# A two-batch encoder layer on one core: the prompt's down-projection joined with the sample's seven products, the sample's convolution as three half-rate filters, the gate's tanh in PSUM

## The chip, the core and the metric

The kernel runs on one core of a Trainium2 chip. A core has a matrix engine (TensorE, PE in the profile), which writes to PSUM, and engines for elementwise work: VectorE (DVE), ScalarE (ACT) and GpSimd (POOL). SyncE (SP) issues most DMA transfers. Each engine takes its own instructions in order and waits on semaphores for the others. The metric is the time of one execution on the device in microseconds; less is better.

## The reference, cut to what matters

One layer of an encoder runs for two batches with the same weights: a prompt of 512 tokens and a sample of 1024. The model width is 1024, the FFN width 2816. Everything is float32.

```python
def _trunk(x, ...):
    h = _rmsnorm(x, norm_attn_g)
    z = h @ w_in                                   # q, k, v, ca, cb
    a_out = _window_attn(q, k, v, bias, band, attn_sink)     # |q-k| <= 128, 8 heads, 2 kv heads
    c = ca * sigmoid(cb)
    c = _dwconv(c, conv_dw_w, conv_dw_b)           # depthwise, 31 taps, 512 channels
    c = silu(_layernorm(c, conv_ln_g, conv_ln_b))
    x = x + concatenate([a_out, c], -1) @ w_out
    h = _rmsnorm(x, norm_ffn_g)
    u = _dwconv(h @ w_up, ffn_dw_w, ffn_dw_b)      # depthwise, 3 taps, 2 * 2816 channels
    x = x + (silu(u[..., :2816]) * u[..., 2816:]) @ w_down
    return _rmsnorm(x, norm_final_g)
y = _trunk(x_prompt, ...), _trunk(x_sample, ...)
```

## The kernel before

**Precision.** Each matrix product is done as three matmuls in a reduced float32 format (F32R): both operands are split into a rounded part `hi` (a copy on ACT) and a rest `lo` (a subtraction on POOL or DVE), and hi x hi, hi x lo and lo x hi are added up in PSUM. A matmul takes 128 rows of the contracted dimension and 512 columns.

**Stages.** The program is one long stream, in this order:

1. Input projections of both batches, weight chunk by weight chunk (`proj`, L288 to L290), with the prompt's convolution and attention mixed in, then the prompt's output projection (`out_half`, L733 to L735).
2. The prompt's FFN: 22 slices of 128 channels (`ffn_step`). A slice has two up-projections of 24 matmuls each (`up_half`), a 3-tap convolution on ACT and DVE (L906, L902), and the gate (`gate`, L920 to L925): tanh on ACT, two steps on DVE or POOL, then the split. Every second slice, `down` multiplies the last two slices with their rows of w_down for 4 blocks of 128 tokens and 2 halves of the width (L940 to L942) and adds each result onto `x1` on DVE (L943). `ffn_end` does the last two slices and normalises and stores the prompt's output.
3. The sample's output projection (blocks of 128 tokens), the norms of its convolution (`conv_norm`, L694 to L717) and the splits of w_out (`split_wo`, L766, L767).
4. The sample's up-projection by a Strassen-Winograd scheme: 7 products of half-size blocks in place of 8 (`first` to `seventh`, all through `prod`, L1167 to L1169). The gate's results and their sums go to DRAM (`ga`).
5. The sample's down-projection by the same scheme: seven products, in the order 1, 2, 5, 6, 7, 4, 3, each over 11 pairs of slices and 4 row blocks (`mm_down`, L1477 to L1479). The operands are loaded back from `ga` and `w_down`, summed and split (`operands`, `split_of`, L1051 to L1055). A product gathers in two wide PSUM tiles of two banks; `evacuate` empties them. There are four wide tiles. The last product is mixed with `finish` (final norm and store).

**Mixing.** In stages 1 and 2 the order is set by counters: `tick()` is called after every two chunks of a projection and after each half block of `down`. Each tick adds `pace["rate"]` to a due count; every full unit advances the generator at the head of `side` by one step (the sample's attention in stage 2, then the loads and splits of w_out, then the first norms). Each tick also adds `pace["late"]` (CD) of credit to the sample's convolution, a generator of single taps.

```python
    pace.update(rate=RD, late=CD)
    for k in range(NJ):
        at[0] = k
        if k == 0:
            side.append(sample())
        ffn_step(k)
    use.update(out=OB, down="b", turn="b")
    pace.update(rate=RE)
    ffn_end(GR[0])
    drain(side)
```

The instructions of an engine are then put in order by a planner that follows this stream by priority with its own estimate of the times; in stage 4 TensorE's order, and in stage 5 TensorE's and SP's, are those of the program. SBUF tiles come from fixed slots (`Slots`), the one that has been free longest first; an instruction that gets a slot waits for its last reader.

**The sample's convolution** (`conv_items`) treats 512 tokens of 128 channels at a time: 24 of the 31 taps on DVE, accumulated in one PSUM bank (L325, L329), 7 as a product on ACT (L317, L320) and an addition on POOL (L321), and a join (L337). Eight such pieces go to DRAM (`cvd`) and are read back block by block by `conv_norm`.

Of the kernel before, what the change touches and what calls it, by code (L numbers as in the profile page):

```python
# [39 lines left out]
RA, RB, RBO, RD, RN, RE = 1.2, 0.8, 2.5, 0.44, 0.8, 0.9  # L40
# [5 lines left out]
NOFF = (4, 7)  # L46

SCB, SCD = "aapa", "vaap"
# [6 lines left out]
FT, PT = 4, (1, 3, 5)  # L55
GP = 1
# [43 lines left out]
def tile_hybrid_encoder(ctx: ExitStack, tc: tile.TileContext, xs, rel_bias, norm_attn_g, w_in,  # L100
# [198 lines left out]
    cvd = {1: dr.tile([P, 4, GR[1]["T"]], F32, name="cvd1")}  # L299
# [4 lines left out]
    def conv_items(g, c, cp):  # L304
        T = GR[g]["T"]
        w = lambda t: cvw[:, t * 4 + c:t * 4 + c + 1]
        cost = 0.13 + NT / 960.0
        noff = NOFF[g]
        off = list(range(CK - noff, CK))
        for n in range(T // NT):  # L310
            src = lambda t: cp[:, t + n * NT:t + (n + 1) * NT]
            pacc = sb.tile([NT])

            def offload(k):
                t = off[k]
                if k == 0:
                    nc.scalar.activation(pacc[:], src(t), AF.Identity, scale=w(t))  # L317
                else:
                    pr = sb.tile([NT])
                    nc.scalar.activation(pr[:], src(t), AF.Identity, scale=w(t))  # L320
                    nc.gpsimd.tensor_tensor(pacc[:], pacc[:], pr[:], op=ALU.add)  # L321

            mid.append((convs, late)[g])
            acc = bank("conv")
            nc.vector.tensor_scalar(acc[:], src(0), w(0), cvb[:, c:c + 1], op0=ALU.mult, op1=ALU.add)  # L325
            yield cost
            k = 0
            for t in range(1, CK - noff):
                nc.vector.scalar_tensor_tensor(acc[:], src(t), w(t), acc[:], op0=ALU.mult, op1=ALU.add)  # L329
                if t % 2 == 1 and k < noff:  # L330
                    offload(k)
                    k += 1
                yield cost
            while k < noff:
                offload(k)
                k += 1
            nc.vector.tensor_tensor(pacc[:], acc[:], pacc[:], op=ALU.add)  # L337
            del acc
            if g == 0:
                kept[c] = pacc  # L340
            else:
                nc.sync.dma_start(cvd[g][:, c, n * NT:(n + 1) * NT], pacc[:])
            mid.clear()
            yield cost

    tanh_t, cpads, kt, vt = {}, {}, {}, {}

    def evac(kind, c, nt, src):
# [9 lines left out]
        elif kind == "ca":  # L358
            if n == 0:
                cp = sb.tile([T + 64])  # L360
                nc.gpsimd.memset(cp[:, 0:PAD], 0.0)
                nc.gpsimd.memset(cp[:, PAD + T:2 * PAD + T], 0.0)
                cpads[g, c] = cp
            cp = cpads[g, c]
            nc.vector.tensor_tensor(src, src, rb[:], op=ALU.mult)
            nc.vector.scalar_tensor_tensor(cp[:, PAD + n * NT:PAD + (n + 1) * NT], tanh_t.pop((nt, c))[:], 1.0, src,
                                           op0=ALU.add, op1=ALU.mult)
# [89 lines left out]
    def landed(i, nt, pp):  # L457
        kind, c, col = order[i]
        evac(kind, c, nt, pp[:])
        if kind == "ca" and nt != 1:  # L460
            g = min(nt, 1)
            (convs, late)[g].append(conv_items(g, c, cpads.pop((g, c))))
        tick()
# [21 lines left out]
    nc.vector.tensor_scalar_mul(cvw[:, :CK * 4], cvw[:, :CK * 4], 0.5)  # L485
    load_rows(1)
# [191 lines left out]
    def conv_norm(i):  # L678
# [6 lines left out]
        else:  # L685
            held = sb.tile([4, P])
            nc.sync.dma_start(held[:], cvd[1][:, :, b * P:(b + 1) * P])
# [23 lines left out]
        for c in range(4):  # L711
            nc.scalar.activation(y[:, c, :], p2[:, c * P:(c + 1) * P], AF.Identity,
                                 scale=lng[:, c:c + 1], bias=lnb[:, c:c + 1])
# [7 lines left out]
    x1d = [dr.tile([P, D], F32, name=f"x1d{i}") for i in range(8)]  # L721

    def out_half(i, n):
# [15 lines left out]
        if n == 1:  # L739
            x1[i] = x  # L740
            if G["g"] == 1:
                nc.sync.dma_start(x1d[i - 4][:], x[:])
# [39 lines left out]
    def make_h2(g, n):  # L782
        ts = []
        for i in range(n * 4, n * 4 + 4):
            k = i if g == 0 else 4 + i
            a = sb.tile([D])
            nc.vector.tensor_scalar_mul(a[:], x1[k][:], rs2[:, k:k + 1])
            ts.append(a)
# [4 lines left out]
    use.update(step="b", turn="a", attn="au", norm="au", out="u")  # L793
# [78 lines left out]
    def want_dn_raw(k):  # L872
        j = seq[k][1]
        dnr[k] = []
        for n in range(2):
            raw = sb.tile([NT])
            nc.sync.dma_start(raw[:], w_down[0, j * P:(j + 1) * P, n * NT:(n + 1) * NT])
            dnr[k].append(raw)

    def want_dn(k):  # L880
        if k in dnr:
            dnw[k] = [split(r) for r in dnr.pop(k)]

# [32 lines left out]
    def gate(ug, uv, pool):  # L916
        gs = []
        for a, b in zip(ug, uv):
            t = sb.tile([NT])
            nc.scalar.activation(t[:], a[:], AF.Tanh, scale=0.5)  # L920
            nc.vector.scalar_tensor_tensor(t[:], t[:], 1.0, a[:], op0=ALU.add, op1=ALU.mult)
            (nc.gpsimd if pool else nc.vector).tensor_tensor(t[:], t[:], b[:], op=ALU.mult)
            hi, lo = sb.tile([NT], F32R), sb.tile([NT], F32R)
            nc.scalar.copy(hi[:], t[:])
            nc.gpsimd.tensor_tensor(lo[:], t[:], hi[:].bitcast(F32), op=ALU.subtract)  # L925
            gs.append((hi, lo))
        return gs

    def down(G, parts, fin):
        base = 4 * G["g"]  # L930
        for tt in range(G["nb"]):
            acc = x1[base + tt]
            c = slice((tt % 4) * P, (tt % 4 + 1) * P)
            for n in range(2):
                pd = bank("down")
                s = slice(n * NT, (n + 1) * NT)
                for x, (gs, wd) in enumerate(parts):
                    hi, lo = gs[tt // 4]
                    wh, wl = wd[n]
                    nc.tensor.matmul(pd[:], hi[:, c], wh[:], start=(x == 0), stop=False)  # L940
                    nc.tensor.matmul(pd[:], hi[:, c], wl[:], start=False, stop=False)
                    nc.tensor.matmul(pd[:], lo[:, c], wh[:], start=False, stop=(x == len(parts) - 1))  # L942
                nc.vector.tensor_tensor(acc[:, s], pd[:], acc[:, s], op=ALU.add)  # L943
                tick()
            if fin is not None:
                ss, rs = sm(2), sm(2)
                o = sb.tile([D])
                for n in range(2):
                    s = slice(n * NT, (n + 1) * NT)
                    nc.scalar.activation(o[:, s], acc[:, s], AF.Square, accum_out=ss[:, n:n + 1])  # L950
                nc.gpsimd.tensor_scalar(rs[:, 0:1], ss[:, 0:1], 1.0 / D, EPS, op0=ALU.mult, op1=ALU.add)
                nc.gpsimd.tensor_scalar(rs[:, 1:2], ss[:, 1:2], 1.0 / D, rs[:, 0:1], op0=ALU.mult, op1=ALU.add)
# [19 lines left out]
    def ffn_step(k):  # L972
# [10 lines left out]
        if j == NJ - 1:  # L983
            want_dn(k)
# [757 lines left out]
```

## Time and profile before

| | |
|---|---|
| median of 3 runs | 1520.96 us (1519.68 to 1521.98) |
| the profiled execution | 1521.1 us, its span 1519.3 us |
| mean granted TensorE clock | 0.997 |
| TensorE busy | 1490.0 us, 98% |
| VectorE, ScalarE, GpSimd busy | 1173.9, 801.8, 737.2 us |
| DMA | 209.71 MB, mean 138 GB/s |

The span runs from the first to the last instruction. Rows of the profile read: line, engine, operation, tile written <- tiles read (names without numbers), shape, count; then the time in which at least one of the group was busy, the mean of one in ns, the engine's idle time before them and who ended it. Tile names are those of the slots: `h` is SBUF of 2048 bytes a partition, `q` of 4096, `c` and `d` others; `a`, `b`, `u`, `c` and `w` are PSUM. Rows of windows give, after the length, the busy time and the count of TensorE, its weight loads, VectorE, ScalarE and GpSimd, then the granted clock, the DMA share and the GB/s. A matmul's own duration overlaps that of the next one.

### The profile page before, as it was taken

Reading aid. Unit: us, or ns where it says so; the run is one execution under the profiler, and the core shown is the slowest. Engines: PE = TensorE matmul, PEld = TensorE weight load, DVE = VectorE, ACT = ScalarE, POOL = GpSimd, SP = SyncE. Lnnn points to the kernel's source line nnn. Section 1 sums busy time; section 2 is a strip of 40 time slices with the busy share of each in tenths; the row PEclk is TensorE's granted clock in tenths of the full one; section 3 lists DMA queues with packets and bytes.
Section 4 is the critical chain, followed back from the end, with each engine's and each line's share of the span. In section 5 each row is a group of like instructions: output and inputs, shape, how many; then the busy total and the mean of one; then the engine's idle time right before and its main releaser. Section 6 shows DMA issues by size and latency. Waiting matters only on the chain. (4 is left out here: it accounts for less than half of the span.)

```text
span 1519.3 us, 20003 instructions
## 1 busy us (share of the span) xinstructions
PE 1490.0 (98%) x6802; PEld 1224.6 (81%) x6802; DVE 1173.9 (77%) x1668; ACT 801.8 (53%) x1419; POOL 737.2 (49%) x649
## 2 busy tenths in 40 slices
PE   8999999899999999999999999999999999999998
PEld 7888778687888778788888888888888888888886
DVE  7877844549999999896575878888888877778794
ACT  6424455447566556655355365544444455454364
POOL 3454353137686777777552325555555554000235
PEclk9999999999999999999999999999999999999999
DMA  9465231823333423335473213333333223396642
GB/s 371 164 166 151 87 101 36 266 97 123 98 112 111 125 91 110 104 113 195 133 258 136 84 56 104 104 105 104 104 105 104 101 94 111 117 393 219 214 146 111
DMA packets 106146, 209.71 MB, mean 138 GB/s; under 512 B 11155, under 2 KB 30739, under 8 KB 105916
## 3 DMA queue, kind: packets, MB, share of 16 engines
q1 hardware_dynamic: 104508, 206.83, 40.9%
q10 hardware_dynamic: 1536, 1.61, 0.3%
q8 instruction: 53, 0.87, 0.2%
q14 instruction: 49, 0.40, 0.1%
HBM read 161.98 MB, written 47.46 MB: 138 GB/s over the span
## 5 line engine op out<-in xcount | busy, mean ns | idle before, releaser
L154 POOL TENSOR_TENSOR q<-q,q 128x1024 fp32r<-128x1024 f32 x66 | 160.2, 2429 | 71.2 <-ACT q L153 34.8
L1051 POOL TENSOR_TENSOR q<-q,q 128x512 fp32r<-128x512 f32 x82 | 114.5, 1408 | 155.7 <-ACT q L1153 151.8
L288 PE MATMUL u<-h,q 128*128 128x512 f32 x384 | 151.7, 395 | 0.1
L290 PE MATMUL u<-h,q 128*128 128x512 f32 x384 | 150.2, 392 | 0.0
L289 PE MATMUL u<-h,q 128*128 128x512 f32 x384 | 150.1, 391 | 0.0
L1167 PE MATMUL w<-h,q 128*128 128x512 f32 x372 | 146.0, 393 | 0.4 <-ACT w L1239 0.4
L1169 PE MATMUL w<-h,q 128*128 128x512 f32 x372 | 144.9, 390 | 0.7 <-POOL q L1051 0.7
L329 DVE SCALAR_TENSOR_TENSOR c<-c,cvw,c 128x512 f32<-128x512 f32 x184 | 137.6, 748 | 1.7
L1168 PE MATMUL w<-h,q 128*128 128x512 f32 x350 | 136.3, 389 | 0.0
L1048 POOL TENSOR_TENSOR q<-q,q 128x1024 f32<-128x1024 f32 x8 | 23.2, 2916 | 177.1 <-DVE q L1048 166.1
L1479 PE MATMUL w<-h,h 128*128 128x512 f32 x264 | 102.7, 389 | 0.0
L1477 PE MATMUL w<-h,h 128*128 128x512 f32 x264 | 102.7, 389 | 0.0
L153 ACT CAST q<-q 128x1024 fp32r<-128x1024 f32 x66 | 69.1, 1050 | 54.6 <-POOL q L154 25.1
L1051 DVE TENSOR_TENSOR h<-h,h 128x512 fp32r<-128x512 f32 (+1 forms) x128 | 89.7, 744 | 9.1 <-ACT h L1055 4.3
L1051 POOL TENSOR_TENSOR c<-q,c 128x512 fp32r<-128x512 f32 x46 | 72.1, 1581 | 49.5 <-ACT c L1153 49.5
L1478 PE MATMUL w<-h,h 128*128 128x512 f32 x244 | 95.1, 390 | 0.6 <-DVE h L1051 0.6
L321 POOL TENSOR_TENSOR h<-h,h 128x512 f32<-128x512 f32 x58 | 76.0, 1311 | 19.5 <-ACT h L320 13.9
L1055 ACT CAST h<-h 128x512 fp32r<-128x512 f32 x101 | 58.9, 618 | 48.6 <-DVE h L1051 27.0
L288 PEld LDWEIGHTS u<-h,q 128*128 128x128 f32 x384 | 72.1, 188 | 15.1 <-DVE h L902 0.6
L1167 PEld LDWEIGHTS w<-h,q 128*128 128x128 f32 x372 | 69.8, 188 | 17.7 <-ACT w L1239 3.7
L290 PEld LDWEIGHTS u<-h,q 128*128 128x128 f32 x384 | 72.1, 188 | 14.7
L289 PEld LDWEIGHTS u<-h,q 128*128 128x128 f32 x384 | 72.2, 188 | 14.0
(459 smaller groups left out, 4355.7 us busy)
## 6 DMA issues: line engine op xcount, KB each, us to landing
q<-in_laid_w_up SPq DMA_DIRECT2D x88, 512.0 KB, 3.6
h<-in_w_down SPq DMA_DIRECT2D x90, 256.0 KB, 3.6
ga<-q SPq DMA_DIRECT2D x65, 256.0 KB, 2.0
h<-ga SPq DMA_DIRECT2D x57, 256.0 KB, 4.3
q<-in_laid_w_in SPq DMA_DIRECT2D x22, 512.0 KB, 4.0
q<-in_x_sample SPq DMA_DIRECT2D x15, 512.0 KB, 6.4
h<-in_laid_w_out SPq DMA_DIRECT2D x28, 256.0 KB, 5.1
h<-qsd SPq DMA_DIRECT2D x24, 256.0 KB, 3.7
```

The lines of the kernel that those rows point to most:

```text
L154: (nc.vector if dve else nc.gpsimd).tensor_tensor(lo[:], raw[:], hi[:].bitcast(F32), op=ALU.subtract)
L288: nc.tensor.matmul(out, whi[:, kc, :], hi[:], start=(kc == 0), stop=False)
L289: nc.tensor.matmul(out, whi[:, kc, :], lo[:], start=False, stop=False)
L290: nc.tensor.matmul(out, wlo[:, kc, :], hi[:], start=False, stop=(kc == KC - 1))
L329: nc.vector.scalar_tensor_tensor(acc[:], src(t), w(t), acc[:], op0=ALU.mult, op1=ALU.add)
L1051: (eng or nc.vector).tensor_tensor(out, a, b, op=ALU.subtract)
L1167: nc.tensor.matmul(out, whi[:, s], hi[:], start=(start and c == 0), stop=False, **go)
L1168: nc.tensor.matmul(out, whi[:, s], lo[:], start=False, stop=False, **go)
L1169: nc.tensor.matmul(out, wlo[:, s], hi[:], start=False, stop=(stop and c == 3), **go)
L1477: nc.tensor.matmul(out, sh[:, c], th[:], start=(p == 0 and not seeded), stop=False, **go)
L1478: nc.tensor.matmul(out, sh[:, c], tl[:], start=False, stop=False, **go)
L1479: nc.tensor.matmul(out, sl[:, c], th[:], start=False, stop=(p == NPAIR - 1), **go)
```

## The change

1. `down` and `ffn_end` are gone. The prompt's gate results go to DRAM (`gap`), in two halves of 256 tokens. While the sample's up-projection runs, `sums_of` forms the sums that the scheme needs from them, on POOL. Each of the seven down products then takes two row blocks of the prompt along (row blocks 4 and 5 in `mm_down`), with a third wide PSUM tile that is opened some steps into the product (`HOLD`; 5 for the first). The prompt's final norm and store move into the last product.
2. The sample's convolution stores its input as even and odd tokens. One filter with the sums of neighbouring taps (16) runs on the odd tokens, two filters (16 and 15 taps) on the differences; each gives 512 outputs and 5 of its taps are offloaded. `conv_norm` puts even and odd outputs back in order.
3. The gate's tanh is written to a PSUM bank, and the step after it works there.
4. Constants: RD 0.44 to 0.55, CAP 48 to 24, and the sample's attention scales one more head on ACT instead of DVE.

```diff
-RA, RB, RBO, RD, RN, RE = 1.2, 0.8, 2.5, 0.44, 0.8, 0.9
+RA, RB, RBO, RD, RN, RE = 1.2, 0.8, 2.5, 0.55, 0.8, 0.9
-SCB, SCD = "aapa", "vaap"
+NOFF = 4
+LOFF = (5, 5, 5)
+SCB, SCD = "aapa", "aaap"
...
+    def late_items(c, cp):
+        odd = lambda m, n=NT: cp[:, 0, m + 1:m + 1 + n]
+        even = lambda m, n=NT: cp[:, 1, m:m + n]
+        ns, no = CK // 2 + 1, CK // 2
+        col = lambda t: cvw[:, t * 4 + c:t * 4 + c + 1]
+        diff = []
+        for k, n in ((0, ns), (1, no)):
+            d = sb.tile([NT + n - 1], among="dq")
+            nc.gpsimd.tensor_tensor(d[:], even(k, NT + n - 1), odd(0, NT + n - 1), op=ALU.subtract)
+            diff.append(d)
+        d = None
+        both = yield from taps(late, odd, lambda s: csum[:, s * 4 + c:s * 4 + c + 1], ns, LOFF[0], with_bias(c))
+        yield 0.13 + NT / 960.0
+        for k, n in ((0, ns), (1, no)):
+            onto = lambda out, x, w: nc.vector.scalar_tensor_tensor(out, x, w, both[:], op0=ALU.mult, op1=ALU.add)
+            y = yield from taps(late, lambda s: diff[k][:, s:s + NT], lambda s: col(2 * s + k), n, LOFF[1 + k], onto)
+            nc.sync.dma_start(cvd[:, c, k, :], y[:])
...
-    def gate(ug, uv, pool):
-        gs = []
-        for a, b in zip(ug, uv):
-            t = sb.tile([NT])
-            nc.scalar.activation(t[:], a[:], AF.Tanh, scale=0.5)
-            nc.vector.scalar_tensor_tensor(t[:], t[:], 1.0, a[:], op0=ALU.add, op1=ALU.mult)
-            (nc.gpsimd if pool else nc.vector).tensor_tensor(t[:], t[:], b[:], op=ALU.mult)
-            hi, lo = sb.tile([NT], F32R), sb.tile([NT], F32R)
...
-    def down(G, parts, fin):
...
-                for x, (gs, wd) in enumerate(parts):
-                    hi, lo = gs[tt // 4]
-                    wh, wl = wd[n]
-                    nc.tensor.matmul(pd[:], hi[:, c], wh[:], start=(x == 0), stop=False)
...
+    def gate(k, a, b):
+        t, pt = sb.tile([2, HT]), bank("gate")
+        nc.scalar.activation(pt[:], a[:], AF.Tanh, scale=0.5)
+        nc.vector.scalar_tensor_tensor(pt[:], pt[:], 1.0, a[:], op0=ALU.add, op1=ALU.mult)
+        nc.vector.tensor_tensor(t[:].rearrange("p h t -> p (h t)"), pt[:], b[:], op=ALU.mult)
+        del pt
+        nc.sync.dma_start(gap[((1, 8), (2, 4))[k % 2]][:, k // 2], t[:])
+
+    def sums_of(p):
+        e, t, x, y = (sb.tile([2, HT]) for _ in range(4))
+        nc.sync.dma_start(e[:], gap[1, 8][:, p])
+        nc.sync.dma_start(t[:], gap[2, 4][:, p])
+        eng = nc.gpsimd
+        eng.tensor_tensor(x[:, 1, :], e[:, 1, :], t[:, 1, :], op=ALU.add)
...
+        nc.sync.dma_start(gap[7, 5][:, p], x[:])
+        nc.sync.dma_start(gap[6, 3][:, p], y[:])
...
-    use.update(out=OB, down="b", turn="b")
+    h2.clear()
+    use.update(out=OB, turn="b")
     pace.update(rate=RE)
-    ffn_end(GR[0])
     drain(side)
...
+        if p % 2 == 0:
+            n = min(2, NPAIR - p) * HT
+            raw = pr.pop((("p", i, 0), p))
+            hi, lo = sb.tile([NT], F32R), sb.tile([NT], F32R)
+            nc.scalar.copy(hi[:, :n], raw[:, :n])
+            sub(lo[:, :n], raw[:, :n], hi[:, :n].bitcast(F32), nc.gpsimd)
+            hp[i, p] = hp[i, p + 1] = hi, lo
...
-    CAP = 48
+    CAP = 24
+    HOLD = 2
     def mm_down(out, i, p, tt, seeded=False):
-        (sh, sl), (th, tl) = hl[i, p]
+        a, (th, tl) = hl[i, p]
         c = slice(tt * P, (tt + 1) * P)
+        if tt > 3:
+            a = hp[i, p]
+            c = slice(p % 2 * HT + (tt - 4) * P, p % 2 * HT + (tt - 3) * P)
...
+        hold = 5 if i == ORDER[0] else HOLD
+        if p == hold:
+            pd.append(wide())
         for tt in range(4):
             mm_down(pd[tt // 2][:, (tt % 2) * NT:(tt % 2 + 1) * NT], i, p, tt)
...
+        if p >= hold:
+            for q in range(p + 1) if p == hold else (p,):
+                for tt in (4, 5):
+                    mm_down(pd[2][:, (tt % 2) * NT:(tt % 2 + 1) * NT], i, q, tt)
+                hl.pop((i, q)), hp.pop((i, q))
```

263 lines of the change are left out of this document (119 added, 144 removed).

## The prediction, on record before the changed kernel ran

> **What bounds the kernel now.** I read, in this order: the page's totals, TensorE's rows one by one, the stages as windows, who waited for whom on TensorE, the groups inside the stage that the diff cuts, and then the seam behind it.
>
> ```profile
> span 1519.3 us, 20003 instructions
> PE 1490.0 (98%) x6802; PEld 1224.6 (81%) x6802; DVE 1173.9 (77%) x1668; ACT 801.8 (53%) x1419; POOL 737.2 (49%) x649
> ...
> 1099.82 0.39 PE L1167 MATMUL w<-h,q 128*128 128x512 f32 x1
> ...
> 1105.94 0.39 PE L1167 MATMUL w<-h,q 128*128 128x512 f32 x1
> ...
> L940 PE MATMUL b<-h,h 128*128 128x512 f32 x144 | 56.5, 396 | 1.7 <-ACT h L153 1.5
> L940 PE MATMUL b<-h,d 128*128 128x512 f32 x32 | 12.8, 405 | 0.2 <-DVE q L943 0.2
> ...
> L1479 PE MATMUL w<-h,h 128*128 128x512 f32 x264 | 102.7, 389 | 0.0
> ```
>
> TensorE is busy 98% of the span, so matmuls are the currency. A matmul lasts 0.39 us but they overlap: from 1099.82 to 1105.94 lie 27 starts, 6.12 / 27 = 0.2267 us each. That, not 0.39, is what one matmul of 512 columns costs the span. L940 stands for the prompt's down-projection: 144 + 32 = 176 rows, and L941 and L942 have as many, 528 matmuls.
>
> ```profile
> 350.00:756.00 406.00, 402.74 (x1868) 332.82 (x1868) 358.31 (x589) 241.69 (x427) 295.37 (x232) 1.00 0.37 120
> 480.00:520.00 40.00, 39.82 (x191) 32.94 (x190) 39.82 (x65) 27.14 (x49) 33.78 (x28) 1.00 0.36 112
> 720.00:756.00 36.00, 36.00 (x163) 29.67 (x161) 16.78 (x23) 12.91 (x20) 19.25 (x12) 1.00 0.37 121
> 1296.00:1513.00 217.00, 216.01 (x951) 177.96 (x949) 167.32 (x228) 104.79 (x193) 40.57 (x37) 1.00 0.57 200
> ...
> PE a L646 <- DVE h L634: 1.6, 2, 1.0
> PE b L940 <- ACT h L153: 1.5, 2, 1.2
> ...
> PE w L1478 <- DVE h L1051: 0.6, 2, 0.3
> ```
>
> The columns after the length are PE, weight load, DVE, ACT, POOL. The prompt's FFN (350 to 756) has a second engine near its limit: DVE 358.31 of 406 us, and all 39.82 of 40 at 480; it is relaxed only after 720, when the attention beside it is over. Yet the waits on TensorE that the profile names are 1 to 2 us a kind there. In the sample's down stage (1296 to 1513) they are 0.6 us in all, with DVE at 167.32 of 217.
>
> **The change, part by part.** *Down-projection.* Removed: 22 slices x 4 row blocks x 2 halves x 3 = 528 matmuls. Added: 7 products x 11 pairs x 2 blocks x 3 = 462. Net 66 x 0.2267 = -15.0 us. 119.7 us go out of the FFN stage, 104.7 come into the last one. Nothing else takes matmuls away, so this is the whole direct gain.
>
> *Work of the other engines in the FFN stage.*
>
> ```profile
> L329 DVE SCALAR_TENSOR_TENSOR c<-c,cvw,c 128x512 f32<-128x512 f32 x184 | 137.6, 748 | 1.7
> ...
> L943 DVE TENSOR_TENSOR q<-b,q 128x512 f32<-128x512 f32 x88 | 59.7, 683 | 13.1 <-PE b L942 12.7
> ...
> L921 DVE SCALAR_TENSOR_TENSOR h<-h,h 128x512 f32<-128x512 f32 x22 | 21.1, 959 | 3.5 <-ACT h L920 3.5
> L922 DVE TENSOR_TENSOR h<-h,h 128x512 f32<-128x512 f32 x16 | 18.3, 1144 | 0.2
> L610 DVE TENSOR_SCALAR h<-h,s 128x384 f32<-128x384 f32 (+1 forms) x13 | 13.4, 1029 | 0.0
> ...
> L154 POOL TENSOR_TENSOR h<-h,h 128x512 fp32r<-128x512 f32 x42 | 55.6, 1328 | 18.0 <-ACT h L153 8.8 <-PE b L941 5.9 <-issue 3.1
> L925 POOL TENSOR_TENSOR h<-h,h 128x512 fp32r<-128x512 f32 x18 | 23.3, 1296 | 8.1 <-ACT h L924 8.1
> L321 POOL TENSOR_TENSOR h<-h,h 128x512 f32<-128x512 f32 x43 | 56.6, 1317 | 8.8 <-PE b L942 3.7 <-ACT h L320 3.5 <-ACT h L317 0.6
> ```
>
> The 88 additions of L943 vanish: -59.7 us of DVE. The convolution has per channel block 2 x 24 taps and 2 joins on DVE now, and 11 + 11 + 10 taps and 3 joins after: 4 x (50 - 35) = 60 operations x 0.75 = -45 us. Its offloaded taps go from 56 to 60 on ACT; POOL keeps 48 additions and gets 8 differences of L321's kind (+11 us). The gate's two DVE steps read PSUM after; the nearest rows with a PSUM input take 0.75 (L329) and 0.68 (L943) against 0.96 and 1.14, so 22 x 1.43 = 31.5 for 39.4: -8 us, though six multiplications come over from POOL. One of the attention's scalings moves from DVE to ACT: some -13 us. DVE: 358 - 60 - 45 - 8 - 13 = 232 us, in a stage of 406 less the share of the 119.7 that lies ahead of 756 (105, the rest stands in the seam below) = 301 us: 77% for 88%. POOL loses the split of w_down and of the gate, 55.6 + 23.3 us. No engine but TensorE bounds the stage on the whole. None of this ends a wait of the span by itself: of TensorE's own waits a few us there are for DVE. I take -2 us; the ends are -6 (its named waits and its longer start-to-start gaps, a few us) and +3 (the same attention now shares 301 us instead of 370, so its chains stand closer).
>
> *The seam behind the FFN.* Ticks count out how the attention is mixed in: 22 x 8 = 176 ticks of the up-projections and 80 of the down-projection, (176 + 80) x 0.44 = 112 steps before; 176 x 0.55 = 96 after. By the code 99 steps of the sample's attention are left at the first slice. So before it ends at slice 19 of 22 (that is the relaxed DVE from 720), after it overhangs by 3 steps, and the split of w_out and the convolution's norm, queued behind it, come when the projections are over.
>
> ```profile
> 754.45 1.66 ACT L766 CAST h<-h 128x512 fp32r<-128x512 f32 x3 [3.54 <-PE u L289]
> ...
> 755.57 0.40 PE L290 MATMUL u<-h,q 128*128 128x512 f32 x1
> ...
> 755.95 0.48 PE L733 MATMUL c<-h,h 128*128 128x512 f32 x1
> ...
> 769.68 0.80 DVE L703 TENSOR_SCALAR h<-a,s,s 128x512 f32<-128x512 f32 x1
> ...
> 777.87 0.68 DVE L717 TENSOR_TENSOR h<-h,h 128x512 fp32r<-128x512 f32 x1
> ...
> 791.52 0.66 DVE L717 TENSOR_TENSOR h<-h,h 128x512 fp32r<-128x512 f32 x1
> ...
> L940 PE MATMUL b<-h,h 128*128 128x512 f32 x16 | 6.4, 401 | 0.0
> ...
> L733 PE MATMUL u<-h,h 128*128 128x512 f32 x8 | 3.1, 390 | 0.0
> ...
> L733 PE MATMUL c<-h,h 128*128 128x512 f32 x5 | 2.2, 431 | 0.0
> ```
>
> The last three rows are groups between 755.7 and 777. Before, the last up-projection matmul starts at 755.57; only then do most splits of w_out find their slots (the ACT split at 754.45 waited for an up-projection). The first norm chain of the sample ends at 777.87 (L717), the second at 791.52. Until the first is there, the output projection can do only the half of its chunks that come from the attention: (8 + 5) x 3 = 39 matmuls (a few are missing; 3 banks x 12 = 36 by the code), 8.2 us of 22. What fills the rest are 16 x 3 = 48 matmuls of the down-projection, 10.9 us, and these are exactly what the change takes away. So TensorE stands open here by up to 777.9 - 755.6 - 8.2 = 14 us, and the second chain gives up to 13.7 us less 48 matmuls (10.9) = 3 more: 17. Against that: ACT and DVE lose the prompt's additions and squares that now stand in front of the chain, the overhanging attention brings TensorE some 2 us, and the planner may draw chains ahead. Lower end 0 (all drawn ahead), upper end 17. I take +8: a chain of 17 us instead of 22, less 8.2 and 2, and 1 to 2 of the second.
>
> A pause has a second price:
>
> ```profile
> PE u L733 <- DVE q L738: 3.2, 1, 3.2
> ...
> 292.00:296.00 4.00, 2.59 (x14) 1.82 (x12) 0.20 (x1) 0.00 (x0) 0.00 (x0) 1.00 1.04 243
> 296.00:300.00 4.00, 0.84 (x3) 0.72 (x3) 1.56 (x6) 0.44 (x2) 0.00 (x0) 0.68 1.00 377
> 300.00:304.00 4.00, 4.00 (x10) 3.08 (x10) 2.25 (x5) 2.27 (x8) 0.00 (x0) 0.50 0.99 383
> ```
>
> After the 3.2 us wait the granted clock (third column from the end) is 0.50 for the 4 us from 300, with 10 matmuls in place of 4 / 0.2267 = 17.6: 7.6 x 0.2267 = 1.7 us lost on top of the idle time. My +8 holds one such loss. [...]
>
> *Last stage.* The stage gets 104.7 us of matmuls for little other work: DVE 167 of 217 before, the same splits and half as many wide additions more over some 322 us. But three wide PSUM tiles per product share four, where two did.
>
> ```profile
> L1048 DVE TENSOR_TENSOR q<-w,q 128x1024 f32<-128x1024 f32 x8 | 9.6, 1216 | 0.0
> ...
> L1504 ACT COPY q<-w x2: 1012/1014/1016, 1390.6 to 1392.2; 128x1024 f32<-128x1024 f32 x2
> ...
> L1553 POOL TENSOR_TENSOR q<-q,q 128x512 f32<-128x512 f32 x6 | 8.6, 1457 | 0.0
> ```
>
> The next product opens with 6 matmuls on the free tile (1.36 us) and then needs one still being emptied, by 1.22 us of DVE or 1.01 of ACT after the last matmul. Near zero when that engine is free, one more 1.2 us each when it isn't: 0 to +7 over six seams; I take +1, nearest to the stage's 0.6 us of waits. The splits for the prompt (42 on ACT and POOL), the sums (44 POOL operations of 256 columns under the sample's up-projection), the gate's stores and some 42 loads more on SP lie beside TensorE at no cost while its queue is fed; CAP halves the loads drawn ahead to 24 tiles, about 9 steps of 4.1 us at 2.5 tiles each, against landings of a few us. If they were late, a step of 4.1 us would open. At the end four blocks instead of two are finished in the last 15 us (66 matmuls): 4 x (1.46 + about 1.1 of small ones) = 10 us of POOL, so 0, at worst +3.
>
> *Sum* against the profiled execution's own 1521.1 us (span 1519.3 and 1.8 around it; the median shown is 1520.96): -15.0 - 2 + 8 + 1 = -8, so **1513 us**.
>
> **Rivals.** *The seam is hidden.* The planner takes the splits and norms into the FFN, which has DVE room at 77%. For: the splits at 712 to 735 of the few that found slots early. Against: the rows above, where the bulk waited for the last up-projection. 1521.1 - 15 - 2 = 1504.
>
> *Slower: the seam stays wide open.* One mechanism: the norm chain of the sample keeps its 22 us and 13.7 us while nothing stands beside it. Price 17, and 2 x 1.7 for two cold starts: 1521.1 - 15 - 2 + 1 + 20.4 = 1525.5. It decides once the seam costs over 19 us (1524). For: what covers it today is what goes. Against: the prompt's own additions, which delay that chain (L703 only at 769.68), go too.
>
> *DVE or the PSUM tiles hold the time.* The filters are moved off an engine that ends few waits, and the three wide tiles cost the full 7: 1513 + 6 = 1519. The conv and gate edits then do nothing, which they nearly do in my sum as well.
>
> **How the numbers follow.** Chances: forecast 0.45, hidden 0.25, open 0.18, PSUM or DVE 0.12. About 0.2% (3 us) is what a measurement can tell from no change: faster means under 1518. Forecast (nearly all) and hidden give 0.67; the rest of the forecast, most of the PSUM case and the lower part of the open one 0.15; slower 0.18. The likeliest alone runs 1508 to 1518; the range takes in the hidden case's 1504 and the edge of the open one, 1503 to 1524.
>
> **What would show it.** Right: 66 matmuls fewer; the FFN stage near 300 us with DVE under 85%; an idle stretch of TensorE of 5 to 10 us just after the last up-projection of the prompt, before the output projection's convolution half, with a dip of the granted clock; the last stage near 320 us with TensorE's waits at product seams under 2 us. Wrong: waits on PSUM evacuations of more than 1 us at each product, a DVE at 95% in the FFN with TensorE waiting for its taps, loads from the new buffers named as releasers, or no gap at all at the seam.

## The result and the profile after

The changed kernel takes 1534.12 us (median of 4 runs, 1531.58 to 1537.43) against 1520.32 us for the kernel before in the same comparison: ratio 1.0091, interval 1.0069 to 1.0113. It is slower by 0.9%; 1513 us was forecast. The profiled execution took 1534.64 us, its span 1532.8 us, 13.5 us longer than before.

The totals and the costliest groups of the page, kernel after:

```profile
span 1532.8 us, 19878 instructions
PE 1487.8 (97%) x6736; PEld 1222.4 (80%) x6736; DVE 1118.8 (73%) x1512; ACT 800.9 (52%) x1417; POOL 764.5 (50%) x683
...
L1468 PE MATMUL w<-h,h 128*128 128x512 f32 x444 | 174.3, 393 | 8.6 <-DVE q L1020 8.1
```

TensorE has 6736 rows for 6802: the 66 matmuls are gone, and DVE lost 55 us. Yet the span grew, and the first line of the product's matmuls (L1477 before, L1468 now) shows the largest part of the reason: 8.1 us of idle time, ended by DVE's wide addition, where the kernel before had 0.0:

```profile
L1477 PE MATMUL w<-h,h 128*128 128x512 f32 x264 | 102.7, 389 | 0.0
```

Windows by stage, kernel after (length; busy time and count of PE, weight loads, DVE, ACT, POOL; clock, DMA share, GB/s): prompt's FFN, seam, sample's up-projection, products.

```profile
366.00:652.00 286.00, 281.94 (x1323) 234.75 (x1324) 239.65 (x418) 194.71 (x351) 192.11 (x159) 0.99 0.47 145
652.00:761.00 109.00, 102.67 (x492) 84.43 (x491) 71.36 (x105) 49.11 (x99) 37.87 (x49) 0.98 0.42 139
761.00:1209.00 448.00, 444.58 (x1970) 363.96 (x1970) 356.08 (x337) 227.40 (x343) 254.75 (x196) 1.00 0.39 129
1209.00:1527.00 318.00, 308.98 (x1348) 253.16 (x1346) 204.67 (x226) 134.84 (x247) 118.47 (x97) 0.99 0.51 171
```

TensorE is open 4.1, 6.3, 3.4 and 9.0 us in these four, by busy time. A finer count takes every distance between two matmul starts. What exceeds 0.2267 us is idle time; where the granted clock is halved (matmuls start 0.42 us apart there, 821.54 to 822.81 in the kernel after), up to another 0.2267 us per matmul is put down as lost to the clock. Idle and half-clock loss by stage, in us:

| stage | before | after | difference |
|---|---|---|---|
| head (to 340 us) | 25.9 + 2.3 | 23.3 + 6.2 | +1.3 |
| prompt's FFN | 16.8 + 0 | 14.6 + 3.7 | +1.5 |
| seam, to the first product | 3.7 + 0 | 9.7 + 1.4 | +7.4 |
| sample's up-projection | 4.7 + 0 | 9.8 + 1.6 | +6.7 |
| the seven down products | 0.9 + 0 | 10.6 + 1.4 | +11.1 |

That is +28.0 in all; with matmul time of -14.0 (by this count; the 66 rows alone give 15.0) and a tail shorter by 0.8 it is +13.2 of the 13.5.

The waits on TensorE, kernel after (engine, what waited, for whom: us in total, times, longest):

```profile
PE w L1468 <- DVE q L1020: 8.1, 4, 2.8
PE a L624 <- DVE h L669: 3.9, 1, 3.9
PE u L770 <- DVE q L775: 3.0, 1, 3.0
PE u L770 <- DVE h L926: 2.9, 1, 2.9
...
PE w L1139 <- ACT q L1125: 2.2, 1, 2.2
...
PE w L1141 <- POOL q L1023: 0.6, 1, 0.6
```

From the top: the product seams; the start of the FFN; a wait at 299 us in the prompt's output projection, which the kernel before has too (3.2); the open seam behind the FFN (L926); and two waits in the up-projection. The first of the product seams in order of time, kernel after (start, us, engine, line; idle time before in brackets):

```profile
1379.65 2.34 DVE L1020 TENSOR_TENSOR q<-w,q 128x1024 f32<-128x1024 f32 x2
...
1380.94 2.37 POOL L1020 TENSOR_TENSOR q<-q,q 128x1024 f32<-128x1024 f32 x1 [1.77 <-DVE q L1020]
...
1381.85 0.39 PE L1470 MATMUL w<-h,h 128*128 128x512 f32 x1
1381.92 1.95 DVE L1023 TENSOR_TENSOR h<-h,h 128x512 fp32r<-128x512 f32 x1
1383.27 1.71 POOL L1023 TENSOR_TENSOR h<-h,h 128x512 fp32r<-128x512 f32 x1
1383.79 1.21 DVE L1020 TENSOR_TENSOR q<-w,q 128x1024 f32<-128x1024 f32 x1
...
1385.05 0.80 PE L1468 MATMUL w<-h,h 128*128 128x512 f32 x1 [2.82 <-DVE q L1020]
```

And the same place as windows:

```profile
1375.00:1381.00 6.00, 6.00 (x28) 4.95 (x28) 3.34 (x4) 2.92 (x5) 1.36 (x2) 1.00 0.58 192
1381.00:1385.00 4.00, 1.23 (x6) 0.69 (x4) 4.00 (x3) 0.00 (x0) 4.00 (x3) 0.97 0.44 137
1385.00:1389.00 4.00, 3.95 (x11) 3.16 (x12) 0.93 (x1) 1.24 (x2) 4.00 (x2) 0.61 0.11 33
```

Two things meet here. The third tile is emptied last (1383.79), but it is the one that the next product needs second: `pd.clear()` drops a list from its end, so the third tile has been free longest by the slot's rule. And ahead of its emptying on DVE stands a split (L1023) of 1.95 us, while POOL runs a wide addition of 2.37. Then 11 matmuls go in 4 us where 17.6 fit (granted clock 0.61). Which of the two costs what, the experiments tell.

### The profile page after: what moved, and what is told of

It reads as the page before. It is cut to its first block, busy times and chain, and to the rows that moved or that the text cites. A ratio compares the mean times of both kernels' runs of the same rounds, so it can differ in the third digit from the quotient of the medians.

```text
span 1532.8 us, 19878 instructions
## 1 busy us (share of the span) xinstructions
PE 1487.8 (97%) x6736; PEld 1222.4 (80%) x6736; DVE 1118.8 (73%) x1512; ACT 800.9 (52%) x1417; POOL 764.5 (50%) x683
## 5 line engine op out<-in xcount | busy, mean ns | idle before, releaser
L1023 DVE TENSOR_TENSOR h<-h,h 128x512 fp32r<-128x512 f32 (+1 forms) x155 | 135.3, 897 | 83.7 <-ACT h L1027 35.0
L1468 PE MATMUL w<-h,h 128*128 128x512 f32 x444 | 174.3, 393 | 8.6 <-DVE q L1020 8.1
L1023 POOL TENSOR_TENSOR q<-q,q 128x512 fp32r<-128x512 f32 x82 | 116.3, 1427 | 116.5 <-ACT q L1125 116.1
L1470 PE MATMUL w<-h,h 128*128 128x512 f32 x436 | 170.3, 391 | 0.0
L1469 PE MATMUL w<-h,h 128*128 128x512 f32 x428 | 167.2, 391 | 0.0
L1027 ACT CAST h<-h 128x512 fp32r<-128x512 f32 x119 | 71.8, 620 | 123.1 <-DVE h L1023 43.7
L1023 POOL TENSOR_TENSOR h<-h,h 128x512 fp32r<-128x512 f32 (+1 forms) x36 | 48.1, 1337 | 173.6 <-ACT h L1451 119.7
L1468 PEld LDWEIGHTS w<-h,h 128*128 128x128 f32 x444 | 83.7, 189 | 28.3 <-DVE q L1020 9.8
L326 DVE SCALAR_TENSOR_TENSOR c<-d,cvw,c 128x512 f32<-128x512 f32 x128 | 96.0, 750 | 1.7
L1470 PEld LDWEIGHTS w<-h,h 128*128 128x128 f32 x436 | 82.2, 188 | 17.2
L1469 PEld LDWEIGHTS w<-h,h 128*128 128x128 f32 x428 | 80.8, 189 | 16.6
L1023 POOL TENSOR_TENSOR c<-q,c 128x512 fp32r<-128x512 f32 x46 | 73.4, 1605 | 36.4 <-ACT c L1125 36.4
L318 POOL TENSOR_TENSOR h<-h,h 128x512 f32<-128x512 f32 x58 | 75.6, 1306 | 22.6 <-ACT h L317 19.1
L289 PEld LDWEIGHTS u<-h,q 128*128 128x128 f32 x384 | 72.7, 189 | 15.9 <-issue 0.9
```

The source lines that it names most:

```text
L289: nc.tensor.matmul(out, whi[:, kc, :], hi[:], start=(kc == 0), stop=False)
L1023: (eng or nc.vector).tensor_tensor(out, a, b, op=ALU.subtract)
L1468: nc.tensor.matmul(out, sh[:, c], th[:], start=(p == 0 and not seeded), stop=False, **go)
L1469: nc.tensor.matmul(out, sh[:, c], tl[:], start=False, stop=False, **go)
L1470: nc.tensor.matmul(out, sl[:, c], th[:], start=False, stop=(p == NPAIR - 1), **go)
```

## The experiments

Edits are against the kernel after, unless said otherwise; the comparison is with the kernel before on the same chip.

**Control: the kernel before, unchanged.**

> The kernel before once more, unchanged. The changed kernel's profile shows nine stretches at half the granted clock (mean 0.988, 0.986 to 0.990 in its four runs), the one of before only one of 6.8 us inside the work (0.997). If such stretches are the luck of where a free-running window falls, this kernel must show 0.990 or less in some of its runs too, and then 5 to 10 us more time. If they belong to the kernel's own pauses, every run is at 0.996 to 0.998 and within 1519 to 1522 us.

1523.41 us over 10 runs, ratio 1.0006 (0.9992 to 1.0019). The ten runs lie between 1517.56 and 1525.02 us with granted clocks of 0.991 to 0.998, which is more spread than the second theory allowed: part of the half-clock loss is luck in this kernel too. But none of the ten comes down to the 0.986 to 0.990 of the changed kernel's four runs. The trace's clock record of the profiled execution (0.997) has two half-clock stretches ahead of the tail, at 160 and 300 us, and nine in the kernel after (0.988): most of them are that kernel's own.

**The order of the tiles.**

```diff
-            pd.clear()
+            while pd:
+                pd.pop(0)
```

> Changed kernel; at the end of a product its wide PSUM tiles are given back first tile first, so the next product's second tile is the one that was emptied first, not the one emptied last. Theory 'product seams' (three waits of 2.3 to 3.0 us on the third tile's evacuation and the half clock behind one of them): 8.3 + 1.4 = 9.7 us less, 1524.5 us, waits of TensorE at the products' ends under 1 us each. Rival 'DVE is simply late' (its splits are slowed by POOL, so any tile comes late): no more than 3 us less, the waits move to the next step.

1531.69 us, ratio 1.0064 (1.0047 to 1.0081). The last stage falls only from 318.5 to 315.7 us, the size that the rival named. Its waits, kernel with the order changed:

```profile
PE w L1469 <- DVE h L1023: 3.0, 1, 3.0
...
PE w L1470 <- POOL d L1023: 1.6, 1, 1.6
PE w L1468 <- ACT h L1451: 1.2, 1, 1.2
...
PE w L1468 <- DVE q L1020: 0.5, 1, 0.5
```

The wait for a tile is down from 8.1 to 0.5, and three others, for operands, open in the last product (1486 to 1491), with a half clock behind them (0.51 over 1492 to 1498). So the order was a cause, and not the only one.

**The sums later.** In `sums_of`'s schedule the first sums come from slice 6, three of them in slices that have one already next to them.

```diff
-        if (j - 2) // 2 < NPAIR and j % 2 == 0:
-            sums_of((j - 2) // 2)
-        if j == NJ - 4:
-            sums_of(NPAIR - 1)
+        if j % 2 == 0 and j >= 6:
+            sums_of((j - 6) // 2)
+        if j in (15, 17, 19):
+            sums_of((j + 1) // 2)
```

> Changed kernel; the prompt's sums begin at slice 6 of the sample's up-projection instead of slice 2. Theory 'the sums come when the up-projection has no lead yet' (idle time of that stage 9.8 us against 4.7, one half-clock stretch of 1.6): 5 to 7 us less, 1528 us, and no wait near 816 us. Rival 'the plan is only another one there': 0 to 2 us less.

1543.55 us, ratio 1.0145 (1.0122 to 1.0169): both theories expected less time, and it is more. The up-projection has 19.1 us of idle time for 9.8. The wait near 816 us is down to 0.76; in the kernel with later sums there is in its place

```profile
PE w L1141 <- POOL q L1023: 7.7, 4, 2.8
```

with three waits of 1.6 to 3.0 us at 1034, 1076 and 1122 us, where sums follow each other slice on slice. The 44 sums are not free under that stage: POOL splits the stage's own operands (L1023), and four more operations in its queue (means of 758 to 1006 ns in the kernel after) make one of these late.

**Denser attention in the FFN.** `RD` 0.55 to 0.62.

> Changed kernel; the attention is mixed into the prompt's FFN at 0.62 steps a tick instead of 0.55, so it ends two slices before the up-projections do. Theory 'open seam behind the FFN' (idle there 9.7 us against 3.7, cold 1.4): 5 us less, 1529 us, with the idle time moved nowhere. Rival 'the FFN has no room for a denser attention': the waits of the FFN stage grow by as much as the seam's shrink, 1534 us or more.

1546.58 us, ratio 1.0164 (1.0144 to 1.0185). The FFN goes from 14.6 + 3.7 to 19.5 + 5.5 us, and the seam does not close: 12.2 + 3.7. In the kernel with 0.62 the longest wait is that of the convolution's norm at the seam (L744, 5.4 us at 669), and waits inside the attention grow (L680, L666):

```profile
PE a L744 <- DVE h L738: 5.8, 2, 5.4
PE a L680 <- ACT h L668: 2.9, 4, 1.2
...
PE a L666 <- DVE s L628: 2.6, 3, 1.2
```

**The old convolution.** The three filters and their layout are taken back; the rest of the change stays. `CD`, 0.65 in both kernels, goes up to 0.8, so that the longer convolution ends inside the shorter FFN.

> Changed kernel with the sample's convolution as it was (31 taps on DVE, ACT and POOL at full rate; its credit 0.8 a tick instead of 0.65, so that it ends inside the shorter FFN). 60 DVE operations of 0.75 us come back, 45 us, into an FFN of 286 us where DVE is busy 240 now. Theory 'the filters are what keeps DVE below TensorE in the shortened FFN': DVE at its limit there, 10 to 30 us more, 1544 to 1564 us. Rival 'the filters lie beside TensorE' (the prediction took them as worth nothing by themselves): 1531 to 1537 us.

1532.9 us, ratio 1.0067 (1.0051 to 1.0082); the interval overlaps that of the kernel after, so the filters gain nothing that can be measured. FFN stage of this kernel:

```profile
340.00:651.00 311.00, 305.06 (x1447) 254.38 (x1447) 292.09 (x518) 219.07 (x396) 205.48 (x171) 0.99 0.45 142
```

Here DVE works 292.09 of 311 us, 94%, and the stage is as long as with the filters (311.3 and 311.4). DVE's sum was no bound.

The filters do show in another stage. In the up-projection, matmuls that read a `c` tile (an SBUF slot) start 233.2 ns apart in the kernel after (mean of 545, pauses of over 0.3 us left out), 226.8 with the old convolution (547) and 226.7 in the kernel before (548); those that read `h` and `q` come 227.9, 226.9 and 227.0 apart. Every kernel here with the filters has the 233. Over 545 and 1079 matmuls this is 4.6 us with no wait behind it, and the stage is 4.3 us shorter with the old convolution. Why matmuls on a `c` tile come further apart stays open: no run varied where the tiles lie.

**The gate's tanh in SBUF again.**

```diff
-        t, pt = sb.tile([2, HT]), bank("gate")
+        t, pt = sb.tile([2, HT]), sb.tile([NT])
```

> Changed kernel with the gate's tanh back in SBUF (the two steps behind it both on DVE). The two DVE steps of the gate take 0.70 and 0.68 us in PSUM, 0.96 and 1.14 in the kernel before. Theory 'off the path': 22 x 0.73 = 16 us more of DVE, time 1531 to 1537 us. Rival 'DVE decides in the shortened FFN': 5 us or more slower.

1538.25 us, ratio 1.0105 (1.0092 to 1.0118). That is 4 us over the kernel after by the medians and 2 by the ratios, whose intervals overlap: a gain of the PSUM tile of a few us is likely, not shown. The FFN has 16.7 + 4.1 us open for 14.6 + 3.7.

**The last stage's small operations on DVE.** Four calls lose their `nc.gpsimd`: the split of the prompt's rows, two additions of `evacuate`, and `with_x`.

```diff
-            sub(lo[:, :n], raw[:, :n], hi[:, :n].bitcast(F32), nc.gpsimd)
+            sub(lo[:, :n], raw[:, :n], hi[:, :n].bitcast(F32))
...
-                add(acc["o12"][w][:], acc["u"][w][:], acc["e"][w][:], nc.gpsimd)
+                add(acc["o12"][w][:], acc["u"][w][:], acc["e"][w][:])
```

> Changed kernel; in the last stage POOL's splits for the prompt (42) and its wide additions (14) go to DVE. Theory 'POOL and DVE hinder each other at SBUF' (DVE's splits take 0.94 us on average there, 0.75 in the kernel before, single ones 1.9 to 2.9 while POOL adds): splits back at 0.75, idle time of the stage 10.6 to 4 us, no half clock, 1526 us. Rival 'DVE has too much to do at the seams': it gets some 48 us more work, the waits grow, 1534 us or more.

1533.54 us, ratio 1.0072 (1.0055 to 1.0089): alone about nothing. But the splits on DVE changed. The groups of DVE in the products' window, in the kernels before, after, with the new order, and with the work on DVE, in that order:

```profile
L1051 DVE TENSOR_TENSOR h<-h,h 128x512 fp32r<-128x512 f32 x85 | 62.8, 774 | 5.3 <-ACT h L1055 4.3 <-DMA h<-ga 0.7
```

```profile
L1023 DVE TENSOR_TENSOR h<-h,h 128x512 fp32r<-128x512 f32 x107 | 99.0, 940 | 54.2 <-ACT h L1027 33.6 <-POOL h L1023 8.0 <-PE w L1470 6.9
...
L1020 DVE TENSOR_TENSOR q<-w,q 128x1024 f32<-128x1024 f32 x12 | 14.4, 1215 | 0.1
```

```profile
L1023 DVE TENSOR_TENSOR h<-h,h 128x512 fp32r<-128x512 f32 x107 | 92.2, 877 | 53.7 <-ACT h L1027 34.7 <-POOL h L1023 10.7 <-PE w L1470 6.8
```

```profile
L1023 DVE TENSOR_TENSOR h<-h,h 128x512 fp32r<-128x512 f32 x132 | 91.0, 705 | 47.8 <-ACT h L1027 33.1 <-PE w L1470 8.2 <-ACT h L1451 4.7
```

132 splits cost less than 107 did, and DVE is no busier in the stage with all that it took over from POOL: 200.50 us for 204.67, while POOL goes from 118.47 to 30.00. Window and wait of the kernel with the work on DVE:

```profile
1213.00:1530.00 317.00, 306.03 (x1331) 251.41 (x1329) 200.50 (x274) 133.62 (x246) 30.00 (x46) 0.99 0.53 174
```

```profile
PE w L1468 <- DVE q L1020: 7.7, 3, 3.6
```

The wait for the tile stays, with short splits: the order is still the old one, and DVE has the additions of POOL in its queue as well.

**Three parts together.** The new order, the work on DVE, and the sums of pairs moved: six of the eleven into the sample's output projection, the other five to every fourth slice of the up-projection.

```diff
             out_blocks(i, n)
+        sums_of(i - 4)
...
-        if (j - 2) // 2 < NPAIR and j % 2 == 0:
-            sums_of((j - 2) // 2)
-        if j == NJ - 4:
-            sums_of(NPAIR - 1)
+        if j % 4 == 0:
+            sums_of(j // 4 + 5)
```

> Changed kernel with three edits: the last stage's POOL work on DVE, the tiles given back first tile first, and the prompt's sums six in the sample's output projection and five at every fourth slice of the up-projection. If the product seams, the contention and the sums' place are independent: last stage's idle time under 2 us (-9 and -1.4 of half clock), up-projection's 9.8 to 5 (-5 and -1.6), 1517 us. If the sums in the output projection delay its norm chains on POOL: the seam grows by about 3 us each, 1521 us or more.

1518.15 us over 12 runs, ratio 0.9971 (0.9961 to 0.9981): faster than the kernel before by 0.3%, and by the two ratios 1.2% faster than the kernel after. The products in this kernel, as a window and by DVE's groups:

```profile
1207.00:1512.00 305.00, 303.16 (x1338) 250.63 (x1336) 201.10 (x276) 134.78 (x247) 34.06 (x46) 1.00 0.54 181
```

```profile
L1023 DVE TENSOR_TENSOR h<-h,h 128x512 fp32r<-128x512 f32 x133 | 90.4, 697 | 45.7 <-ACT h L1027 31.0 <-PE w L1471 7.3 <-ACT h L1452 6.3
...
L1020 DVE TENSOR_TENSOR q<-w,q 128x1024 f32<-128x1024 f32 x12 | 14.4, 1218 | 0.0
```

The granted clock is 1.00, and no wait of TensorE on this stage's operands or tiles of 0.2 us or more is left in its list.

**Two of the three, without the sums.**

> The three-part kernel (1518.15 us) without its move of the sums of pairs: only the order in which the product's tiles are given back and the last stage's small operations on VectorE are changed against the kernel after. Theory one: the two act together in the last stage alone, because each leaves the other's wait standing (either one alone left 7.4 or 9.7 us idle there); then the last stage falls to about 305 us with under 1 us idle, the stage of up-projections stays near 433 us with about 10 us idle, and the time is 1518.2 + 4 to 6 = 1522 to 1524 us. Theory two: the sums, early or late, are what disturbs the queues of the last stage too; then it keeps more than 5 us idle and the time stays at 1528 us or more.

1521.26 us over 11 runs, ratio 0.9989 (0.9979 to 0.9999); products 304.7 us with -0.4 + 0 us open (nothing, within the count), up-projection 433.9. Theory one, 0.7 us below its time: the two act in the last stage alone, and each hides the other's gain. Of the 12.0 us open in that stage the order alone took 2.7 (7.4 + 1.9 left), the work on DVE alone nothing (9.7 + 3.0 left), both together all. In the ratio that is 0.0027, 0.0019 and 0.0102. Whether what was left behind the new order went because DVE's splits are shorter, or because POOL's own late split (1.6 us there) is gone, was not tried apart.

**The sums alone.**

> The kernel after with nothing but the sums of pairs moved: six of them to the stretch of attention outputs behind the joined stage, the other three spaced four slices apart. Theory one: the wait behind the sums in the up-projection stage is its own term of 3 to 6 us (the stage falls from 433.8 to 428 to 431 us with no half clock, as it did in the three-part kernel), the last stage keeps its 10 us idle: 1528 to 1531 us. Theory two: these waits are only shifted into the stretch of outputs before the products, whose POOL work delays the norms: the seam grows beyond its 108.9 us by as much and the time stays at 1533 to 1536 us.

(The expectation speaks of three other pairs; the kernel moves five.) 1532.26 us, ratio 1.0065 (1.005 to 1.0081). The up-projection fell to 430.0 us with no half clock and the seam stayed (109.1), as theory one had it; the products lost more to the clock (4.4 for 1.4), and the time is 1 us above the forecast. On top of the pair the same move takes the stage from 433.9 to 429.9 us and the median from 1521.26 to 1518.15. Its size is shown by the stage; in the whole time the intervals of both pairs of runs still touch.

**Thinner attention on top of the three parts.** `RD` 0.50.

> The three-part kernel with the density of the attention work in the joined stage at 0.50 instead of 0.55. Theory one: the joined stage's idle (14.4 us) and half clock (3.0 us) come from VectorE being loaded too densely (denser, at 0.62, they were 19.5 and 5.5 us); then thinner work gives 2 to 5 us there and the seam behind it gives back about as much or less, 1513 to 1519 us. Theory two: what doesn't fit in the joined stage is done at its end with nothing beside it, so the seam grows by more than the stage saves: 1520 to 1526 us.

1532.16 us, ratio 1.0068 (1.0056 to 1.008): the side of theory two, 6 us beyond its upper end. The FFN is 4.0 us shorter (309.7 to 305.7), but no stall went: idle time and half clock together stay within 0.5 us, and the stage has 27 matmuls of the attention fewer, which come at the seam. That goes from 110.3 to 127.9. With fewer steps of attention done in the FFN, TensorE has 18.7 + 7.6 us open at the seam for 9.4 + 3.0. With 0.62 also dearer (there on the kernel after), 0.55 lies between two steep sides.

**The gate alone, on the kernel before.** The same tile in PSUM, in one of the two banks of `b`; six of the 22 last multiplications move from POOL to DVE with it.

> The kernel before with one part of the change alone: the gate's tanh and its first product stand in a PSUM bank, the third operation stays on VectorE. The attention of the two groups keeps its place. Theory one: the part is worth about 1 us here, because the work lies beside a stage that TensorE fills, 1518 to 1522 us. Theory two: the tanh read from PSUM relieves SBUF's side of VectorE as it did in the kernel after (without it that was 4 us slower): 1514 to 1518 us. A bank taken from another use could as well cost: above 1523 us.

1557.89 us, ratio 1.0237 (1.0219 to 1.0255), far out of both theories and on the side of the third possibility. The gate's two steps on DVE do get shorter, and now TensorE waits in the FFN. Waits, then groups, of the kernel with the gate alone:

```profile
PE b L941 <- DVE q L944: 7.9, 8, 2.0
PE u L288 <- DVE h L902: 7.8, 6, 2.4
```

```profile
L921 DVE SCALAR_TENSOR_TENSOR b<-b,h 128x512 f32<-128x512 f32 x22 | 15.2, 694 | 4.2 <-ACT b L920 4.1
L922 DVE TENSOR_TENSOR h<-b,h 128x512 f32<-128x512 f32 x22 | 15.1, 686 | 0.3
```

The two steps took 959 and 1144 ns before. The FFN has 42.0 + 6.0 us open for 16.8. The longest of the named waits is the down-projection's (L941), which gathers in `b` too and waits for its own addition (L944) to empty a bank. That the gate holds a bank that it lacks is a reading; no run varied the count of banks. In the kernel after that user of `b` is gone; if the reading holds, the gate's tile could be moved only together with the down-projection.

## Why the prediction was wrong

**What failed: the term for the product seams, +1, measured +11.1.** The mechanism stood there ("six matmuls on the free tile, then one still being emptied") and so did its sign of failure, "waits on PSUM evacuations of more than 1 us at each product". The size was off twice. It took one emptying of 1.2 us as the most that a seam can cost, and did not ask which tile is asked for second: it is the one emptied last, behind two others and a split. The three long seams cost 2.98, 2.35 and 2.97 us beyond the usual distance of matmul starts (at 1381.85, 1431.35 and 1481.46). And it took "nearest to the stage's 0.6 us of waits", a row of a stage with two tiles and little POOL work (40.57 us; 118.47 after).

**What failed: "the splits for the prompt, the sums ... lie beside TensorE at no cost".** The splits and additions on POOL lengthen DVE's own (774 to 940 ns). Moving them to DVE shows little while the old order stands, and the new order little while they stay; with both mended no wait is left. The sums cost about 4 of the +6.7 in the up-projection: in the three kernels with most of them early the stage has 7.5 to 7.6 + 0 us open; the kernel after and the one without that move have 9.8 + 1.6 and 10.0 + 1.5. What stays is no wait: it goes with the filters, by the 233.2 ns between matmuls on `c` tiles. With the old convolution and the sums late the stage had 5.7 + 1.5, with the same two pauses near 820 us. The prediction had no term for either.

**What was missing: the clock.** One half-clock loss of 1.7 us was in the sum, in the seam; the stretch before that it was read from lasts 6.8 us by the clock record and costs 2.3. By the table 12.0 us more than before are lost to half clock, in nine stretches for one (3.9 more in the head, 3.7 in the FFN). The longest is at the start of the FFN. DVE's queue there, and then windows, kernel after:

```profile
362.82 3.92 DVE L326 SCALAR_TENSOR_TENSOR c<-c,csum,c 128x512 f32<-128x512 f32 x5
366.66 1.40 DVE L926 SCALAR_TENSOR_TENSOR h<-u,fw,h 128x511 f32<-128x511 f32 x2
367.97 0.68 DVE L334 TENSOR_TENSOR h<-c,h 128x512 f32<-128x512 f32 x1
368.57 0.68 DVE L669 TENSOR_TENSOR h<-a,h 128x512 fp32r<-128x512 f32 x1
```

```profile
365.00:369.50 4.50, 0.63 (x6) 0.39 (x4) 4.43 (x8) 4.50 (x8) 4.01 (x3) 0.78 0.63 226
369.50:372.00 2.50, 2.50 (x7) 1.89 (x8) 2.50 (x3) 0.84 (x2) 2.19 (x1) 0.50 0.02 7
```

Five taps in a row keep DVE 3.92 us, two steps of the FFN's own convolution and a join follow, and only then comes L669, for which the attention waits (L624, 3.9), with the up-projections behind it; 7 matmuls go in the 2.5 us from 369.5, where 11 fit. ACT's copy for L669 ends at 367.56, so DVE's queue is not the whole of it. Why the pause is there stays open. The kernel with the old convolution has one of 3.1 us at 368, the one with `RD` 0.50 one of 3.8 at 365, so neither of these edits alone removes it. The missing down-projection is not it: in the kernel before its first matmul starts at 374.85, and no pause from 340 to 400 us is over 1.2. The head's loss varies between kernels with the same head (6.2 here, 3.4 in the three-part kernel, 2.6 with the new order; 2.3 and 3.1 in two profiles of the kernel before), so part of its +3.9 is no cost of the change.

**What was right.** The direct gain: 66 rows fewer. The FFN: from 350 to the last up-projection at 651.45 it is 301 us, as forecast, with DVE at 84%, under the 85 named, if above the 77 worked out. Its stalls eased by 2.2 us (forecast 2), and the clock took 3.7 back. The seam's size and place: forecast +8 with one half clock, measured +7.4 with one, just behind the last up-projection. Windows of the kernel after, then rows of its timeline:

```profile
652.00:656.00 4.00, 1.17 (x9) 0.69 (x7) 3.73 (x5) 3.95 (x9) 1.62 (x2) 1.00 1.05 405
656.00:660.00 4.00, 2.87 (x8) 2.32 (x9) 3.54 (x7) 1.85 (x5) 3.49 (x5) 0.71 1.10 379
660.00:664.00 4.00, 3.07 (x13) 2.24 (x12) 0.82 (x2) 2.32 (x5) 3.56 (x3) 0.86 0.93 326
664.00:668.00 4.00, 2.57 (x15) 2.12 (x16) 2.91 (x6) 3.99 (x9) 2.89 (x4) 1.00 0.74 246
```

```profile
651.45 0.39 PE L291 MATMUL u<-h,q 128*128 128x512 f32 x1
...
657.13 0.47 PE L770 MATMUL u<-h,h 128*128 128x512 f32 x1 [2.93 <-DVE h L926]
```

```profile
670.16 0.65 DVE L754 TENSOR_TENSOR h<-h,h 128x512 fp32r<-128x512 f32 x1
```

The first chain (L754) ends 19 us after the last up-projection, near the 17 of the sum. But the +7.4 is partly luck. The sum let the attention's half of the output projection start at once and put 6.8 us of idle time behind it, for the first chain. Here that half itself starts late: it waits 2.9 us, up to 657.13, for DVE's 3-tap convolution of the last slice (L926), which still reads a bank of `u`. Pauses before the norm's transposes (L729) cost less than 3 us from 662 to 667, and from 668 on TensorE is busy all of 9 us, while the chain still runs. The filters were worth nothing measurable, as the rival with DVE off the path said, and in the list of waits no load from the new buffers is named.

**The rivals.** "Seam open" gave 1525.5 and slower: the side was right, the mechanism was not, since the seam cost 7.4. That it pays for two cold starts was the author's estimate; the kernel after shows one half clock at the seam, 1.4 us. "Hidden" fell with it. "DVE or the PSUM tiles" named the place, with at most 7 us and a chance of 0.12. With those two causes mended, the three-part kernel's 1518.15 is still 5 us above the forecast (3.7 by its ratio to the kernel before). By its stages, against before: FFN +0.6 (14.4 + 3.0), seam +8.7 (9.4 + 3.0), up-projection +2.8, products -1.3, head +0.5. Most of the 5 is the FFN's half clock and the rest of the up-projection.

## What to carry to other kernels

When more tiles of a ring are emptied at a seam, write down the order in which they come free and the order in which they are asked for next; the price is that of the last emptying with its queue, not of one operation (here 2.98, 2.35 and 2.97 us of pause for an emptying of 1.2). Work put "beside" the matrix engine is free only if it delays nothing on its own engine that TensorE waits for (with the sums later, 7.7 us for POOL's splits): look at the queue of each engine at the seams. And a part that does nothing alone can be half of a pair: of 12.0 us, one edit took 2.7, the other none, both took all.

## What the hardware showed that was not expected

**POOL slows DVE.** The same split takes 774 ns before, 940 with POOL 118.47 us busy in the stage, and 697 with POOL at 34.06. DVE's wide addition with one input in PSUM (L1020) is 1216, 1215 and 1218: not touched. The splits' mean is longer by a third (940 for 697), with 1.95 us for the one that held the seam. Sorted one by one, the 107 splits of the kernel after say the same: the 69 with POOL idle beside them take 677 to 695 ns, the 32 with POOL busy for more than half of their time 1531 on average and up to 2900. Why the splits are slowed and the addition is not was not shown.

**A half clock follows short pauses, but not each.** By the trace's clock record the pause of 2.98 us at 1381.85 was followed by a half clock (0.61 over the next 4 us), those of 2.35 and 2.97 us at 1431 and 1481 were not; at 816 and 819 two pauses of 2.38 and 0.79 us were followed by one at 821.5. The half-clock stretches of this kernel are 3.4 us long, one 6.8, and they come after single pauses shorter than that as well (2.97 us at 653.93, 2.98 at 1381.85). The nine begin at whole multiples of 3.413 us from the first (44, 82, 86, 99, 105, 190, 238 and 403 steps later). What sets apart the pauses that a half clock follows was not shown: no run moved a pause.

**A gain on one engine, a loss of 36 us.** In the kernel before, the gate's steps get shorter by 265 and 458 ns (959 and 1144 to 694 and 686), and the time rises from 1522.32 to 1557.89 us.
